# A hybrid mLSTM and neighbourhood-attention block: the z projection channel-major, the conditioning sums in PSUM, the first score blocks spaced, the gate chain split

## The chip, the core and the metric

The kernel runs on one core of one Trainium2 chip. The core has a matrix engine (PE, TensorE), a vector engine (DVE), a scalar engine (ACT), GpSimd (POOL) and a queue engine (SP) that issues most of the DMAs. SBUF is the main on-chip memory; matmuls write into eight banks of PSUM. The metric is the device time of one execution in microseconds (us); lower is better.

## What is computed

One layer over 1024 tokens of width 1024. Every product of real size is done at about float32 accuracy.

```python
cond = silu(c)
shift, scale, gate = split(cond @ w_ada + b_ada, 3)
h = rms_norm(x, norm_gain) * (1 + scale) + shift
proj = h @ w_in          # q_a k_a v_a o_a z_a (1024 each), 16 gates, q_b k_b v_b z_b (512 each), g_merge (2048)
# branch A: 4 heads of 256, bidirectional chunkwise mLSTM
q_a, k_a = split(silu(centred_dwconv(concat(q_a, k_a))))
h_a = sigmoid(o_a) * bidirectional_mlstm(q_a, k_a, v_a, gates)
y_a = rms_norm_per_head(h_a, mlstm_norm_gain) * silu(z_a)
# branch B: 8 heads of 64, neighbourhood attention on a 16 x 64 grid
y_b = neighbourhood_attention(q_b, k_b, v_b, rpb) * silu(z_b)
gm = sigmoid(g_merge + b_merge)
merged = gm[:, 0] * (y_a @ w_proj_a) + gm[:, 1] * (y_b @ w_proj_b)
out = rms_norm(x + gate * (merged @ w_out), final_gain)
```

## The kernel before, in words

Every float32 operand of a large product is split into a rounded high part and a low remainder, and a product is three matmuls: high by high, high by low, low by high (`mm3`). ACT writes the high part, POOL or DVE subtracts it for the low part. `wraw` is a raw weight tile, `whi` and `wlo` its parts, `hhi` and `hlo` the parts of the normalised activations h, kept with channels on the partitions.

A dense product has two forms. The channel-major form (`dense_cm`, and `dense_cm_steps` in the front) holds a 128x128 weight tile stationary and moves 512 tokens past it, so a matmul has 512 columns and the result has channels on the partitions. The token-major form (`dense_tm`) holds 128 tokens of h stationary and moves 256 weight columns, so a matmul has 256 columns and the result has tokens on the partitions. For 256 output channels and the 8 slices of h's channels the first takes 8 x 2 x 2 x 3 = 96 matmuls of 512 columns, the second 8 x 8 x 3 = 192 of 256. Each uses four PSUM banks called `dps`; four more, tag `m`, serve everything small.

The program has five stages.

1. The front (`front`, L239) loads x and the conditioning weights w_ada, normalises and transposes x, and forms shift and scale for eight bands k of 128 channels. For each band a running sum `acc` over eight slices of w_ada is made on DVE (`mod_acc`, L275), one instruction per slice, and PE sums it over the partitions with a matmul against ones (`mod_sum`, L288). `split_at` says how many of the eight slices go through DVE; the others go to PE as matmuls of one column each. `mod_out` makes the vectors `md`, `h_tile` (L329) applies them and writes hhi and hlo. In the same loop PE computes the first query and key projection (`dense_cm_steps`) and the gate projection (`gate_step`, tile `gaps`), band by band. The order of DVE and ACT is written out by hand here, as is that of PE everywhere.
2. Neighbourhood attention (`na_chain`, L692). A chain of 64 blocks (scores, softmax, transposed weights, values) is woven into a stream of dense work. `weave` keeps a count of PE time; each `yield x` of a chain says after how much PE time its next piece may go. The tile `sps` with the scores has a single PSUM buffer, which DVE frees when it writes the normalised weights `pt` (L772).
3. The projection of branch B (`projb`, L833): first one merge gate product (`gmerge`, whose eviction on ACT writes `gtmp`, L828, and sends it to DRAM as `t_d`), then four groups of w_proj_b. Beside it runs the chain `gates` (L502), which makes the mLSTM's decay vectors: scans on DVE up to `M`, `negM` (L543), its copy to DRAM (L544), the decays `dec` on ACT (L547) and their DMAs (L548, L549), and then four vectors that PE transposes (tile `gps`).
4. Branch A (`branch_a`): per head the products k, v, q, then for the head before it `gated_out` (L1068): the o and z products, both token-major. o's eviction multiplies the mLSTM's output `hout`, sums its squares, and after the fourth of four evictions one call of `rsqrt` makes the eight normalising factors `hrstd` (a power on POOL, L236). z's eviction makes `sz` = silu(z) times the normalised hout, and `y_out` (L1097) transposes it, multiplies by the gain and writes it to DRAM (or, for the last head, into the tiles `ya`). The chain of the mLSTM is woven into this stream.
5. The products with w_proj_a and w_out, and the final norm.

Outside the front a scheduler of the framework chooses the order of ACT, DVE, POOL and SP from the program's order and the data's dependences; PE keeps the program's order.

Of the kernel before, what the change touches and what calls it, by code (L numbers as in the profile page):

```python
# [12 lines left out]
F32 = mybir.dt.float32  # L13
F32R = mybir.dt.float32r
AF = mybir.ActivationFunctionType
ALU = mybir.AluOpType
# [3 lines left out]
P = 128  # L20
T = 1024
D = 1024
NK = 8
HEADS = 4
# [17 lines left out]
def f32(ap):  # L42
    return ap.bitcast(F32)


class Build:
# [192 lines left out]
    def front(self, cols):  # L239
# [3 lines left out]
        with self.pool("fr", bufs=2) as fp:  # L243
            wv = io["w_ada"].rearrange("(p j) (s k n) -> p j s k n", j=8, s=3, k=8)
            was, w, xts, accs, md, rs = [], [], [], [None] * NK, [], []
            half = [slice(0, 512), slice(512, T)]

            def load_wa(k):
# [21 lines left out]
                for _ in range(n):  # L270
                    self.transpose(ps, self.ident, self.ident)

            split_at = [8, 0, 8, 7, 8, 8, 8, 8]

            def mod_acc(k, j0, j1):  # L275
                if j0 == 0:
                    accs[k] = fp.tile([P, 2, P], F32, name="acc", bufs=3)
                    nc.vector.tensor_scalar_mul(accs[k], was[k][:, 0], self.cs[:, 0:1])
                for j in range(max(j0, 1), min(j1, split_at[k])):
                    nc.vector.scalar_tensor_tensor(accs[k], was[k][:, j], self.cs[:, j:j + 1], accs[k], op0=ALU.mult, op1=ALU.add)  # L280

            def mod_mix(k, js):
                for j in js:
# [45 lines left out]
            def h_tile(k, s):  # L329
                x, hi, lo, m = xnT[:, k, s], self.hhi[k][:, s], self.hlo[k][:, s], md[k]  # L330
                nc.scalar.activation(x, x, AF.Identity, scale=m[:, 1:2], bias=m[:, 0:1])
                nc.scalar.activation(hi, x, AF.Copy)
                nc.gpsimd.tensor_tensor(lo, x, f32(hi), op=ALU.subtract)  # L333

            def h_high(s):
                x, m = xnT[:, 0, s], md[0]
# [91 lines left out]
            mod_whole(1, 0)  # L428
            copy(7, True)
            mod_whole(1, 1)  # L430
            keep_warm(4, self.psm, "m")
            h_high(half[1])
            split_w(1)
# [66 lines left out]
    def gates(self, gp):  # L500
# [36 lines left out]
        def natural(src, fac):  # L537
            n = gp.tile([36, T], F32, name="nat", bufs=2)
            nc.vector.tensor_scalar_mul(n, src, fac)
            nc.vector.tensor_scalar_mul(n[32:36, ::-1], src[32:36, :], fac)  # L540
            return n
        negM = gp.tile([36, T], F32, name="negM")
        nc.vector.tensor_scalar_mul(negM, M, -1.0)  # L543
        nc.scalar.dma_start(self.negm_d, natural(negM, 1.0))  # L544
        dec = gp.tile([36, NCH], F32, name="dec")
        for c in range(NCH):
            nc.scalar.activation(dec[:, c:c + 1], negM[:, c * L + L - 1:c * L + L], AF.Exp, bias=mc[:, c:c + 1])  # L547
        nc.scalar.dma_start(dec_d, dec)  # L548
        nc.scalar.dma_start(self.decb, dec_d.rearrange("a b -> (a b)").partition_broadcast(P))  # L549
        for i in range(4):  # L550
            if i == 0:
                q = u
            else:
                q = gp.tile([36, T], F32, name="gq", bufs=2)
            if i == 3:
                nc.vector.tensor_tensor(q, b, M, op=ALU.add)
                nc.scalar.activation(q, q, AF.Exp, scale=-1.0)
            for c in range(NCH):
                s = slice(c * L, c * L + L)
                if i == 1:  # L560
                    nc.scalar.activation(q[:, s], u[:, s], AF.Exp, bias=negM[:, c * L + L - 1:c * L + L])
                if i == 2:
                    nc.scalar.activation(q[:, s], negM[:, s], AF.Exp, bias=mc[:, c:c + 1])
            n = natural(q, (1.0, 1.0 / 32, 0.5, 1.0)[i])
            yield 21.0 if i == 0 else 5.0
            ps = self.psm.tile([P, 512], F32, name="gps", tag="m")
            for tt in range(8):
                self.transpose(ps[:, tt * 36:(tt + 1) * 36], n[:, tt * P:(tt + 1) * P], self.ident[0:36, 0:36])
            nc.vector.tensor_copy(self.col[i].rearrange("p a b -> p (a b)"), ps[:, 0:288])
# [116 lines left out]
    def na_chain(self):  # L686

        n = 4 * 16
        heads = {}
        for i in range(n + 3):  # L690
            if i < n:
                pair, hh, b = i // 16, i // 8 % 2, i % 8  # L692
                if b == 0:
                    if hh == 0:
                        if pair == 0:
                            heads[0] = self.na_head(0, 0)
                        yield f"qk{pair}"
                        yield 12.0 if pair == 0 else 6.0
                if (hh, b) == (0, 1) or (hh, b) == (1, 4) and pair < 3:
                    heads[i // 8 + 1] = self.na_head(pair + hh, 1 - hh)  # L700
                self.na_scores(heads[i // 8], b)
                if i % 16 == 15:
                    self.flags.add(f"S{pair}")
                yield NLAG
            if 1 <= i <= n:
                self.na_weights(heads[(i - 1) // 8], (i - 1) % 8)
                yield NLAG
            if i >= 3:
                j = i - 3
                pair = j // 16  # L710
                if j % 16 == 0:
                    yield f"v{pair}"
                    yield 3.2
                    st = self.na_pair[pair]
                    st["v"] = self.np_.tile([P, 8, 2, 2, 64], F32R, name="vb")
                    for h in range(2):
                        self.na_vprep(st, h)
                        yield 1.3
                    yield 1.3
                self.na_values(heads[j // 8], j % 8)  # L720
                if j % 16 == 15:
                    self.flags.add(f"na{pair}")
                yield NLAG
# [312 lines left out]
    def ml_scores(self, mp, c, qh, kh, hd, Pm):  # L1036
# [11 lines left out]
        for dr, row in ((0, rowf), (1, rowb)):  # L1048
# [15 lines left out]
                nc.vector.scalar_tensor_tensor(Dm[:, 1:3], sfl[:, 2:4], 1.0 / 64, Dm[:, 1:3], op0=ALU.mult, op1=ALU.mult)  # L1064
            Pm.append((blocks, self.split(mp, [P, 3, P], Dm, "pm", bufs=2)))

    def gated_out(self, mp, hd):

        nc, io = self.nc, self.io
# [4 lines left out]
        def ev_o(b, ps):  # L1074
            for i in range(2):
# [2 lines left out]
                nc.scalar.activation(so, ps[:, i], AF.Tanh, scale=0.5)  # L1078
                nc.vector.scalar_tensor_tensor(hout[:, tt], so, 1.0, hout[:, tt], op0=ALU.add, op1=ALU.mult)
                nc.scalar.activation(so, hout[:, tt], AF.Square, accum_out=ssq[:, tt:tt + 1])  # L1080
            if b == 3:
                self.rsqrt(rstd, ssq, 1.0 / HD, 4 * EPS, mp, 8)

        def ev_z(b, ps):
            if b % 2 == 0:
                self.sz = mp.tile([P, 2, 2, 256], F32, name="sz", tag="up", bufs=2)
            sz = self.sz[:, b % 2]
            nc.scalar.activation(sz, ps, AF.Tanh, scale=0.5)
            nc.vector.scalar_tensor_tensor(sz, sz, 1.0, ps, op0=ALU.add, op1=ALU.mult)
            for i in range(2):  # L1090
                tt = 2 * b + i
                nc.vector.scalar_tensor_tensor(sz[:, i], hout[:, tt], rstd[:, tt:tt + 1], sz[:, i], op0=ALU.mult, op1=ALU.mult)
            self.spawn(self.y_out(mp, hd, b, sz))
        yield from self.dense_tm(io["w_in"], [(OA + hd * 256, 256)], self.htok, ev_o)
        yield from self.dense_tm(io["w_in"], [(ZA + hd * 256, 256)], self.htok, ev_z)

    def y_out(self, mp, hd, b, sz):  # L1097
        nc = self.nc
        yield 5.0
        tp = self.psm.tile([P, 2, 2, P], F32, name="ytp", tag="m")  # L1100
        for i in range(2):
            for dt in range(2):
                self.transpose(tp[:, dt, i, :], sz[:, i, dt * P:(dt + 1) * P], self.ident)
        s = slice(b * 256, (b + 1) * 256)
        last = hd == HEADS - 1
        if not last:
            yt = mp.tile([P, 2, 256], F32, name="yt", bufs=2)
        for dt in range(2):
            k = hd * 2 + dt
            gain = self.mgain[:, k:k + 1]  # L1110
            if last:
                hi, lo = self.ya[k]
                nc.scalar.activation(hi[:, s], tp[:, dt], AF.Copy, scale=gain)
                nc.vector.scalar_tensor_tensor(lo[:, s], tp[:, dt], gain, f32(hi)[:, s], op0=ALU.mult, op1=ALU.subtract)
            else:
                nc.scalar.activation(yt[:, dt], tp[:, dt], AF.Copy, scale=gain)
                nc.scalar.dma_start(self.ya_d[k][:, s], yt[:, dt])
        if b == 3:
            self.flags.add(f"y{hd}")

    def ml_fill(self, mp):
        gm = [[2], [], [], [3]]
        for hd in range(HEADS):
            yield from self.qkv(mp, hd)
            if hd:
                yield from self.gated_out(mp, hd - 1)
            for g in gm[hd]:
                yield from self.gmerge(0, g)
        yield "ml3"
        yield from self.gated_out(mp, 3)  # L1130

    def branch_a(self):

        nc, io = self.nc, self.io
        with ExitStack() as fs:
# [1 line left out]
            mp = ms.enter_context(self.pool("ml"))  # L1137
            self.mmask = mp.tile([P, 2, P], F32, name="mmask")
            nc.scalar.dma_start(self.mmask, io["mask_ml"])
            self.ml_head = {}  # L1140
            self.spawn(self.ml_chain(mp))

            def fill():
# [193 lines left out]
```

## Time and profile before

| what | value |
|---|---|
| time, median of 3 runs | 1309.07 us (1308.64 to 1310.47) |
| the profiled execution's own time | 1309.19 us |
| its span in the profile | 1307.4 us |
| PE busy | 98% of the span |
| DVE, ACT, POOL busy | 49%, 43%, 32% |

The span runs from the first instruction to the last; the time has 1.8 us more, which lie around it. Matmuls overlap, so a matmul's duration in a row is longer than the distance to the next one. That a PE is 98% busy therefore does not say that it is at its peak. PEclk is the granted clock of TensorE: 1.00 stands for 2.4 GHz and 0.50 for 1.2 GHz.

### The profile page before, as it was taken

How to read it: one execution, taken by the hardware profiler on the slowest of the kernel's cores; microseconds unless marked ns; L12 is line 12 of the kernel's file. 1: busy time of each engine (PE TensorE's matmuls, PEld its weight loads, DVE VectorE, ACT ScalarE, POOL GpSimd, SP SyncE). 2: the span in 40 equal slices, each digit the busy share in tenths (PEclk: the TensorE clock that was granted, in tenths of full speed). 3: DMA queues.
4: the chain of work that ended last, by engine and by line, in shares of the span. 5: the costliest groups of instructions: out<-in, count | busy, mean ns of one | idle time of the engine just before them, and what ended most of it. 6: DMA issues, size and time to landing. Idle time of an engine off the chain costs nothing.

```text
span 1307.4 us, 19858 instructions
## 1 busy us (share of the span) xinstructions
PE 1283.6 (98%) x7560; PEld 1129.6 (86%) x7560; DVE 640.5 (49%) x1381; ACT 564.9 (43%) x1191; POOL 418.0 (32%) x383
## 2 busy tenths in 40 slices
PE   8899999999999999999999999999999999999997
PEld 7678888888888789889989989999989989888886
DVE  6944536445354523356546653465545641533433
ACT  6564435444355313345435543365435543423222
POOL 2653534334346123122212122232212122252332
PEclk9899999999999899999999999999999999999999
DMA  9632222312223462122111221112111123456432
GB/s 291 155 92 83 83 67 82 85 46 84 65 82 129 142 201 60 36 73 49 42 41 41 66 62 44 41 50 71 44 41 41 55 79 93 146 156 202 142 109 85
DMA packets 106187, 116.24 MB, mean 89 GB/s; under 512 B 9724, under 2 KB 86012, under 8 KB 106092
## 3 DMA queue, kind: packets, MB, share of 16 engines
q1 hardware_dynamic: 97352, 102.69, 27.3%
q10 hardware_dynamic: 8740, 12.29, 2.7%
q8 instruction: 59, 0.97, 0.3%
q14 instruction: 36, 0.29, 0.1%
HBM read 92.48 MB, written 20.08 MB: 86 GB/s over the span
## 4 chain that ended last, share of the span: by engine, by line
PE 90%; DVE 4%; DMA 2%; ACT 1%; issue 1%; SPq 1%; POOL 0%; POOLq 0%; ACTq 0%; DVEq 0%
PE dps L79 67%; PE ops L79 8%; PE ips L79 5%; PE sps L79 3%; PE cps L79 3%; PE tps L83 1%; DVE acc L280 1%; DMA t_d<-gtmp 1%; DMA wa<-in_w_ada 1%; PE kps L83 1%; PE ytp L83 0%; SPq L251 0%; DVE M L532 0%; DMA xt<-in_x 0%; DMA ya<-ya_d 0%
## 5 line engine op out<-in xcount | busy, mean ns | idle before, releaser
L74 POOL TENSOR_TENSOR wlo<-wraw,whi 128x512 fp32r<-128x512 f32 x168 | 227.8, 1356 | 577.5 <-ACT whi L73 576.6
L79 PE MATMUL dps<-hhi,whi 128*128 128x512 f32 x768 | 311.8, 406 | 0.8 <-ACT hhi L338 0.5
L79 PE MATMUL dps<-hhi,wlo 128*128 128x512 f32 x768 | 302.6, 394 | 0.0
L79 PE MATMUL dps<-hlo,whi 128*128 128x512 f32 x768 | 299.4, 393 | 0.2 <-POOL hlo L333 0.2
L79 PE MATMUL dps<-whi,hhi 128*128 128x256 f32 x768 | 217.5, 283 | 0.0
L79 PE MATMUL dps<-whi,hlo 128*128 128x256 f32 x768 | 217.4, 283 | 0.0
L79 PE MATMUL dps<-wlo,hhi 128*128 128x256 f32 x768 | 217.4, 283 | 0.0
L73 ACT ACTIVATE whi<-wraw 128x512 fp32r<-128x512 f32 x168 | 105.6, 629 | 229.6 <-PE dps L79 184.6
L79 PEld LDWEIGHTS dps<-hhi,wlo 128*128 128x128 f32 x768 | 145.1, 189 | 32.0
L79 PEld LDWEIGHTS dps<-hhi,whi 128*128 128x128 f32 x768 | 145.5, 189 | 20.2 <-issue 1.7
L79 PEld LDWEIGHTS dps<-hlo,whi 128*128 128x128 f32 x768 | 145.2, 190 | 19.7 <-POOL hlo L333 1.5
L79 PEld LDWEIGHTS dps<-whi,hhi 128*128 128x128 f32 x768 | 147.2, 192 | 0.2
L79 PEld LDWEIGHTS dps<-wlo,hhi 128*128 128x128 f32 x768 | 147.1, 192 | 0.2
L79 PEld LDWEIGHTS dps<-whi,hlo 128*128 128x128 f32 x768 | 147.1, 192 | 0.0
L79 PE MATMUL dps<-ya,whi 128*128 128x512 f32 x256 | 79.4, 392 | 0.0
L769 ACT ACTIVATE sps<-pt,mx 128x384 f32<-128x384 f32 (+1 forms) x64 | 35.7, 558 | 89.8 <-DVE mx L767 89.8
L79 PEld LDWEIGHTS dps<-ya,whi 128*128 128x128 f32 x256 | 47.7, 188 | 9.8 <-DVE t0r L1183 0.3
L1053 POOL TENSOR_TENSOR dg<-negm,mmask 128x256 f32<-128x256 f32 x32 | 24.5, 765 | 98.3 <-issue 28.6
L79 PE MATMUL ops<-woh,mhi 128*128 128x512 f32 (+1 forms) x136 | 51.4, 378 | 0.0
L79 PE MATMUL ops<-woh,mlo 128*128 128x512 f32 (+1 forms) x136 | 51.3, 377 | 0.0
L79 PE MATMUL ops<-wol,mhi 128*128 128x512 f32 (+1 forms) x136 | 51.3, 377 | 0.0
L79 PE MATMUL dps<-ya,wlo 128*128 128x512 f32 x128 | 49.9, 390 | 0.0
(266 smaller groups left out, 2345.8 us busy)
## 6 DMA issues: line engine op xcount, KB each, us to landing
wraw<-in_w_in SPq DMA_DIRECT2D x112, 256.0 KB
wa<-in_w_ada SPq DMA_DIRECT2D x16, 512.0 KB
wraw<-in_w_in SPq DMA_DIRECT2D x64, 128.0 KB
t_d<-gtmp ACTq DMA_DIRECT2D x32, 256.0 KB
xt<-in_x SPq DMA_DIRECT2D x8, 512.0 KB
wag<-in_w_ada SPq DMA_DIRECT2D x16, 256.0 KB
t1r<-t_d SPq DMA_DIRECT2D x8, 512.0 KB
mp_d<-t1r SPq DMA_DIRECT2D x16, 256.0 KB
```

What stands on the lines that cost most here:

```text
L73: nc.scalar.activation(hi, raw, AF.Copy)
L74: nc.gpsimd.tensor_tensor(lo, raw, f32(hi), op=ALU.subtract)
L79: self.nc.tensor.matmul(out, lhsT=lhsT, rhs=rhs, start=start, stop=stop, skip_group_check=True)
L83: self.nc.tensor.transpose(out, src, ident)
L280: nc.vector.scalar_tensor_tensor(accs[k], was[k][:, j], self.cs[:, j:j + 1], accs[k], op0=ALU.mult, op1=ALU.add)
L769: nc.scalar.activation(sv, p_, AF.Exp, bias=mx, scale=-1.0, accum_out=sm)
L1053: nc.gpsimd.tensor_tensor(dg, negm.rearrange("p (a b) -> p a b", a=2), mk, op=ALU.add)
```

## The change

It has four parts, called A to D from here on.

A. In the front, the bands 4 to 7 give their eighth slice to PE (two more one-column matmuls each, one for shift and one for scale). The running sums of the bands from 2 on are kept in a PSUM tile `accp`, one half for even and one for odd bands; the last step of a sum writes the SBUF tile `acc`. The low parts of the bands 6 and 7 are subtracted on DVE and no longer on POOL.

B. In the gate chain a wait of 24 us of PE time stands before negM, and the later 21 is 8. The three DMAs of negM and dec are issued from SP's queue and no longer from ACT's.

C. The chain of neighbourhood attention leaves 2.4, 1.8 and 1.2 us after its first three score blocks, where it left 0.6.

D. z is computed channel-major, before o, into a tile `sz` of its own. rsqrt is called after each of o's evictions, for two factors, and ACT scales hout by them. `y_out` transposes hout, 10 us of PE time later (before: 5), and DVE multiplies the transposed tile by gain and sz.

```diff
-            split_at = [8, 0, 8, 7, 8, 8, 8, 8]
+            split_at = [8, 0, 8, 7, 7, 7, 7, 7]
...
                     accs[k] = fp.tile([P, 2, P], F32, name="acc", bufs=3)
-                    nc.vector.tensor_scalar_mul(accs[k], was[k][:, 0], self.cs[:, 0:1])
+                    parts[k] = run[0][:, k % 2] if k > 1 else accs[k]
+                    nc.vector.tensor_scalar_mul(parts[k], was[k][:, 0], self.cs[:, 0:1])
                 for j in range(max(j0, 1), min(j1, split_at[k])):
-                    nc.vector.scalar_tensor_tensor(accs[k], was[k][:, j], self.cs[:, j:j + 1], accs[k], op0=ALU.mult, op1=ALU.add)
+                    out = accs[k] if j == split_at[k] - 1 else parts[k]
+                    nc.vector.scalar_tensor_tensor(out, was[k][:, j], self.cs[:, j:j + 1], parts[k], op0=ALU.mult, op1=ALU.add)
...
-                nc.gpsimd.tensor_tensor(lo, x, f32(hi), op=ALU.subtract)
+                (nc.vector if k > 5 else nc.gpsimd).tensor_tensor(lo, x, f32(hi), op=ALU.subtract)
...
+            run.append(self.psm.tile([P, 2, 2, P], F32, name="accp", tag="m"))
...
+        yield 24.0
         negM = gp.tile([36, T], F32, name="negM")
         nc.vector.tensor_scalar_mul(negM, M, -1.0)
-        nc.scalar.dma_start(self.negm_d, natural(negM, 1.0))
+        nc.sync.dma_start(self.negm_d, natural(negM, 1.0))
...
-        nc.scalar.dma_start(dec_d, dec)
-        nc.scalar.dma_start(self.decb, dec_d.rearrange("a b -> (a b)").partition_broadcast(P))
+        nc.sync.dma_start(dec_d, dec)
+        nc.sync.dma_start(self.decb, dec_d.rearrange("a b -> (a b)").partition_broadcast(P))
...
-            yield 21.0 if i == 0 else 5.0
+            yield 8.0 if i == 0 else 5.0
...
-                yield NLAG
+                yield NLAG if i > 2 else 2.4 - NLAG * i
...
+    def z_path(self, mp, hd):
+        nc, io = self.nc, self.io
+        def evac(a, h, banks):
+            if a == 0 and h == 0:
+                self.sz[hd] = mp.tile([P, 2, T], F32, name="sz", tag="sz")
+            sz = self.sz[hd][:, a, h * 512:h * 512 + 512]
+            nc.scalar.activation(sz, banks[h], AF.Tanh, scale=0.5)
+            nc.vector.scalar_tensor_tensor(sz, sz, 1.0, banks[h], op0=ALU.add, op1=ALU.mult)
+        yield from self.dense_cm(io["w_in"], [(ZA + hd * 256, 256)], self.hT, evac)
...
-            if b == 3:
-                self.rsqrt(rstd, ssq, 1.0 / HD, 4 * EPS, mp, 8)
-
-        def ev_z(b, ps):
...
-                nc.vector.scalar_tensor_tensor(sz[:, i], hout[:, tt], rstd[:, tt:tt + 1], sz[:, i], op0=ALU.mult, op1=ALU.mult)
-            self.spawn(self.y_out(mp, hd, b, sz))
+            s = slice(2 * b, 2 * b + 2)
+            self.rsqrt(rstd[:, s], ssq[:, s], 1.0 / HD, 4 * EPS, mp, 2)
+            for tt in (2 * b, 2 * b + 1):
+                nc.scalar.activation(hout[:, tt], hout[:, tt], AF.Copy, scale=rstd[:, tt:tt + 1])
+            self.spawn(self.y_out(mp, hd, b, hout))
...
-        yield 5.0
+        yield 10.0
...
-                self.transpose(tp[:, dt, i, :], sz[:, i, dt * P:(dt + 1) * P], self.ident)
+                self.transpose(tp[:, dt, i, :], hout[:, 2 * b + i, dt * P:(dt + 1) * P], self.ident)
...
+            nc.vector.scalar_tensor_tensor(yt[:, dt], tp[:, dt].rearrange("p i t -> p (i t)"), gain, self.sz[hd][:, dt, s], op0=ALU.mult, op1=ALU.mult)
             if last:
                 hi, lo = self.ya[k]
-                nc.scalar.activation(hi[:, s], tp[:, dt], AF.Copy, scale=gain)
-                nc.vector.scalar_tensor_tensor(lo[:, s], tp[:, dt], gain, f32(hi)[:, s], op0=ALU.mult, op1=ALU.subtract)
+                nc.scalar.activation(hi[:, s], yt[:, dt], AF.Copy)
+                nc.vector.tensor_tensor(lo[:, s], yt[:, dt], f32(hi)[:, s], op=ALU.subtract)
             else:
-                nc.scalar.activation(yt[:, dt], tp[:, dt], AF.Copy, scale=gain)
                 nc.scalar.dma_start(self.ya_d[k][:, s], yt[:, dt])
```

In `ml_fill` the call of `z_path` for a head stands right before its `gated_out`, which now does o alone; that of the last head stands before the hold `"ml3"`, which waits for the last mLSTM chunk.

On DVE in the front, the sums of the bands 3 to 5 before (`acc` is the running sum of a band, `md` a band's finished vectors; the sums of two bands take turns):

```order
L280 SCALAR_TENSOR_TENSOR acc<-wa,cs,acc 128x256 x6
L278 TENSOR_SCALAR acc<-wa,cs 128x256
L303 TENSOR_TENSOR md<-mps,b_ada_c_sb 128x1
L304 SCALAR_TENSOR_TENSOR md<-mps,b_ada_c_sb 128x1
L305 TENSOR_TENSOR md<-md,norm_gain_sb 128x1
L280 SCALAR_TENSOR_TENSOR acc<-wa,cs,acc 128x256 x7
```

The same place after the change, and at the end the last sum of band 7 with what follows it:

```order
L283 SCALAR_TENSOR_TENSOR accp<-wa,cs,accp 128x256 x3
L280 TENSOR_SCALAR accp<-wa,cs 128x256
L306 TENSOR_TENSOR md<-mps,b_ada_c_sb 128x1
L307 SCALAR_TENSOR_TENSOR md<-mps,b_ada_c_sb 128x1
L308 TENSOR_TENSOR md<-md,norm_gain_sb 128x1
L283 SCALAR_TENSOR_TENSOR accp<-wa,cs,accp 128x256 x2
L283 SCALAR_TENSOR_TENSOR acc<-wa,cs,accp 128x256
...
L283 SCALAR_TENSOR_TENSOR acc<-wa,cs,accp 128x256
L336 TENSOR_TENSOR hlo_103<-xnT,hhi_102 128x512 x2
```

A band has seven sum instructions rather than eight, six of them without two SBUF operands; the two subtractions for band 6 stand behind the last sum.

On ACT where branch B's projection begins, before (`dec` needs negM, `gq` is the second gate vector, the DMA of `negm_d` needs the tile `nat`):

```order
L547 ACT_TABLE_LOAD
L547 ACTIVATE dec<-negM,mc 36x1 x4
L561 ACTIVATE gq<-gate_4124,negM 36x256
L548 DMA dec_d<-dec 36x4
L544 DMA negm_d<-nat 36x1024
L828 ACTIVATE gtmp<-dps,bmh 128x512
L549 DMA decb<-dec_d 128x144
L829 DMA t_d<-gtmp 128x512
L828 ACTIVATE gtmp<-dps,bmh 128x512
```

And after the change:

```order
L552 ACT_TABLE_LOAD
L552 ACTIVATE dec<-negM,mc 36x1 x4
L566 ACTIVATE gq<-gate_4129,negM 36x256
L833 ACTIVATE gtmp<-dps,bmh 128x512 x2
L834 DMA t_d<-gtmp 128x512 x2
```

The three DMAs are gone from the queue; the four `dec` and the first `gq` still stand ahead of the first `gtmp`. On PE the transposes of the first gate vector, which stood behind 6 matmuls of w_proj_b, stand behind 60.

On ACT around o's evictions of the last head, before (`so` is sigmoid's tanh, the second instruction squares hout):

```order
L1078 ACTIVATE so<-dps 128x256 x2
L1080 ACTIVATE so,hssq<-hout 128x256 x2
```

And after:

```order
L1095 ACTIVATE so<-dps 128x256 x2
L1097 ACTIVATE so,hssq<-hout 128x256 x2
L1095 ACTIVATE so<-dps 128x256 x2
L1101 ACTIVATE hout<-hout,hrstd 128x256 x2
```

Two scalings of hout per eviction, which need the power on POOL, now stand in ACT's queue between the evictions.

## Rows read from the trace of the kernel before

**Rows 1.** The page's first part: busy time, share of the span, instructions.

```profile
PE 1283.6 (98%) x7560; PEld 1129.6 (86%) x7560; DVE 640.5 (49%) x1381; ACT 564.9 (43%) x1191; POOL 418.0 (32%) x383
```

**Rows 2.** PE's waits: waiting instruction, releaser, us in total, times, longest.

```profile
PE mps L291 <- DVE acc L280: 6.3, 5, 2.1
PE sps L79 <- DVE pt L772: 2.5, 3, 1.2
PE dps L79 <- ACT gtmp L828: 1.8, 1, 1.8
```

**Rows 3.** The chain that ended last, in time order: start, us, what.

```profile
20.13 7.25 DMA wa<-in_w_ada
...
146.86 16.33 PE dps L79 x72
...
1077.44 42.85 PE dps L79 x358
```

**Rows 4.** PE's timeline in the front: start, us, instruction, idle before and releaser.

```profile
39.17 0.38 PE L291 MATMUL mps<-ones,acc 128*128 128x1 f32 x2 [1.93 <-DVE acc L280]
...
47.02 0.50 PE L291 MATMUL mps<-ones,acc 128*128 128x1 f32 x4
...
58.03 0.61 PE L291 MATMUL mps<-ones,acc 128*128 128x1 f32 x4 [2.07 <-DVE acc L280]
58.50 0.47 PE L79 MATMUL gaps<-hhi,gw 128*128 128x512 f32 x1
...
63.48 0.61 PE L291 MATMUL mps<-ones,acc 128*128 128x1 f32 x4 [1.07 <-DVE acc L280]
...
73.58 0.39 PE L79 MATMUL dps<-hhi,whi 128*128 128x512 f32 x1
```

**Rows 5.** DVE instructions by tile: ns min/median/max, first and last start.

```profile
L280 DVE SCALAR_TENSOR_TENSOR acc<-wa,cs,acc x48: 472/484/1523, 13.4 to 62.9; 128x256 f32<-128x256 f32 x48
...
L1092 DVE SCALAR_TENSOR_TENSOR sz<-hout,hrstd,sz x32: 467/479/1530, 739.7 to 1128.6; 128x256 f32<-128x256 f32 x32
...
L1089 DVE SCALAR_TENSOR_TENSOR sz<-sz,dps x16: 672/684/690, 738.9 to 1125.7; 128x512 f32<-128x512 f32 x16
```

**Rows 6.** DVE's timeline in the front.

```profile
44.02 4.93 DVE L280 SCALAR_TENSOR_TENSOR acc<-wa,cs,acc 128x256 f32<-128x256 f32 x7
```

**Rows 7.** POOL's timeline over the same stretch.

```profile
45.69 2.97 POOL L333 TENSOR_TENSOR hlo<-xnT,hhi 128x512 fp32r<-128x512 f32 x2 [2.07 <-ACT hhi L332]
```

**Rows 8.** SP's timeline: an issue of w_ada, and the first after branch B's weights.

```profile
29.52 1.76 SPq L251 DMA_DIRECT2D wa<-in_w_ada  x1
...
446.73 0.34 SPq L852 DMA_DIRECT2D mp_d<-t1r  x1
```

**Rows 9.** Two windows: us, busy PE, PEld, DVE, ACT, POOL, PEclk, DMA, GB/s.

```profile
39.50:46.40 6.90, 6.90 (x21) 5.65 (x21) 6.79 (x13) 3.99 (x7) 4.72 (x4) 0.51 1.14 284
435.50:442.30 6.80, 6.80 (x22) 5.05 (x22) 1.47 (x3) 4.18 (x9) 0.00 (x0) 0.50 0.59 164
```

**Rows 10.** PE's timeline at the second and third score blocks.

```profile
88.81 0.44 PE L79 MATMUL sps<-kB,qA 128*128 128x384 f32 x1 [1.18 <-DVE pt L772]
...
91.78 0.45 PE L79 MATMUL sps<-kB,qA 128*128 128x384 f32 x1 [0.75 <-DVE pt L772]
```

**Rows 11.** ACT's timeline where branch B's projection begins.

```profile
434.24 0.69 ACT L828 ACTIVATE gtmp<-dps,bmh 128x512 f32<-128x512 f32 x1 [1.14 <-DVE nat L540]
...
434.95 0.37 ACTq L829 DMA_DIRECT2D t_d<-gtmp  x1
...
439.00 0.69 ACT L828 ACTIVATE gtmp<-dps,bmh 128x512 f32<-128x512 f32 x1 [2.55 <-DMA t_d<-gtmp]
```

**Rows 12.** PE's timeline at the same place.

```profile
434.98 0.50 PE L79 MATMUL dps<-ybhi,whi 128*128 128x512 f32 x1 [1.82 <-ACT gtmp L828]
```

**Rows 13.** A window of branch A, ACT alone: us, busy ACT, PEclk, DMA, GB/s.

```profile
683.00:780.00 97.00, 51.79 (x126) 1.00 0.20 55
```

**Rows 14.** POOL's timeline at the last head's normalising factors.

```profile
1103.89 1.65 POOL L236 TENSOR_TENSOR hrstd<-rsq,mhalf 128x8 f32<-128x8 f32 x1
```

More of the change, by code (lines that the diff above doesn't have):

```diff
@@ L245, in front @@
             was, w, xts, accs, md, rs = [], [], [], [None] * NK, [], []
+            parts, run = [None] * NK, []
             half = [slice(0, 512), slice(512, T)]
@@ L1080, in ev_o, with y_out @@
                 nc.scalar.activation(so, hout[:, tt], AF.Square, accum_out=ssq[:, tt:tt + 1])
-            if b == 3:
-                self.rsqrt(rstd, ssq, 1.0 / HD, 4 * EPS, mp, 8)
-        def ev_z(b, ps):
[L1085 to L1091, printed above, removed]
-                nc.vector.scalar_tensor_tensor(sz[:, i], hout[:, tt], rstd[:, tt:tt + 1], sz[:, i], op0=ALU.mult, op1=ALU.mult)
-            self.spawn(self.y_out(mp, hd, b, sz))
+            s = slice(2 * b, 2 * b + 2)
[3 more added lines that the diff above has]
+            self.spawn(self.y_out(mp, hd, b, hout))
         yield from self.dense_tm(io["w_in"], [(OA + hd * 256, 256)], self.htok, ev_o)
-        yield from self.dense_tm(io["w_in"], [(ZA + hd * 256, 256)], self.htok, ev_z)
-    def y_out(self, mp, hd, b, sz):
+    def y_out(self, mp, hd, b, hout):
         nc = self.nc
-        yield 5.0
+        yield 10.0
         tp = self.psm.tile([P, 2, 2, P], F32, name="ytp", tag="m")
@@ L1102, in y_out @@
             for dt in range(2):
-                self.transpose(tp[:, dt, i, :], sz[:, i, dt * P:(dt + 1) * P], self.ident)
+                self.transpose(tp[:, dt, i, :], hout[:, 2 * b + i, dt * P:(dt + 1) * P], self.ident)
         s = slice(b * 256, (b + 1) * 256)
         last = hd == HEADS - 1
-        if not last:
-            yt = mp.tile([P, 2, 256], F32, name="yt", bufs=2)
+        yt = mp.tile([P, 2, 256], F32, name="yt", bufs=2)
         for dt in range(2):
@@ L1125, in ml_fill @@
             if hd:
+                yield from self.z_path(mp, hd - 1)
                 yield from self.gated_out(mp, hd - 1)
@@ L1128, in ml_fill @@
                 yield from self.gmerge(0, g)
+        yield from self.z_path(mp, HEADS - 1)
         yield "ml3"
@@ L1139, in branch_a @@
             nc.scalar.dma_start(self.mmask, io["mask_ml"])
-            self.ml_head = {}
+            self.ml_head, self.sz = {}, {}
             self.spawn(self.ml_chain(mp))
```

## The prediction, made before the changed kernel ran

> **What bounds the kernel now.** The page's first part comes first: PE is busy 98% of the span, the other engines about half of it or less [rows 1]. So only three kinds of change can pay: fewer PE microseconds, less PE idle time, or a higher clock. Next come PE's waits by releaser: DVE's sums in the front cost 6.3 us in five waits, the first score blocks 2.5 in three, one eviction in branch B's projection 1.8 [rows 2]. The chain of waits runs through PE nearly throughout. Its long pieces give the true distance of matmuls, since the duration of one overlaps the next: 16.33/72 = 0.2268 us for 512 columns, 42.85/358 = 0.1197 for 256 [rows 3]. Windows come last: in two stretches of about 6.9 us the granted clock is half, 1.2 rather than 2.4 GHz [rows 9]. Each follows a PE wait (1.93 us until 39.17, 1.82 until 434.98) [rows 4, 12], and each gives away about half its length, 3.4 us.
>
> **Part A, the front.** The five waits are for `acc`. A sum instruction takes 0.48 us at the median but up to 1.52 [rows 5]; seven of them took 4.93 us while POOL wrote hlo for 2.97 us [rows 6, 7]. The tile list points at the cause: `sz` at L1092, whose two large inputs are both in SBUF, reaches 1.53 us, while L1089, on twice the columns but with one input in PSUM, never exceeds 0.69 [rows 5]. With the running sum in PSUM I expect the long ones to go. The new instruction itself is not shown: 0.35 from below (half of 0.69), 0.69 from above; I take 0.48, the same step on SBUF.
>
> From the sum matmul at 58.03 to that at 63.48 lie 5.45 us, of which 1.07 are idle and about 0.16 the drain of the last matmul (0.39 long, 0.23 apart): 4.2 us of PE work per band [rows 4]. The two sums of a band cost 58.50 - 58.03 = 0.47; two more matmuls of that size make a band 4.7 us on PE. DVE has seven sum steps and three short ones, 7 x 0.48 + 0.4 = 3.8, so PE sets the pace unless a step exceeds about 0.62.
>
> The earlier waits stay: band 4's weights, issued at 29.52 [rows 8], land after about 7.25 us [rows 3], near 36.8, and DVE's first product of band 4 stands in its queue ahead of band 2's vectors, with or without the change. Hence I expect PE idle until about 38.9 again, the half clock after it, and the sum of band 4 at about 46.8 (now 47.02). From there three bands at 4.7 reach band 7's sum at 60.9 (now 63.48). Its own two added matmuls cost 0.47, and the 10.1 us to the next dense product (63.48 to 73.58) [rows 4] stay: it starts at 71.5, or at 70.8 if the small waits in those 10.1 go too. Gain 2.1 to 2.8; I take 2.5. Lower end: the long steps stay, the bands keep today's pace and the 0.47 comes on top, gain -0.5. Upper end: the clock no longer falls, 2.5 + 3.4 = 5.9. The subtractions of bands 6 and 7 stand on DVE behind the last sums; POOL took 1.48 us for one [rows 7], DVE's form with two SBUF operands 0.48 for half the columns, so h is ready no later and they cost nothing; if DVE were late there, the front's last products would wait about 1 us, which the lower end covers.
>
> **Part C, the score blocks.** The second block's scores wait 1.18 us for the single score bank, the third's 0.75; their distance is 2.97 us [rows 10], and the three waits add to 2.5 [rows 2]. Now 12 matmuls of 0.2268 stand between the first two blocks in place of 3, as many between the next two and 9 between the two after them: 2.7 us, with the block's own 0.45 more than 2.97, and 2.0 with scores and transposes about 2.9. Gain 2.4 (2.0 to 2.5). The dense work spent here is missing later in the chain, where PE has no such wait; if it runs out there, up to 2.4 comes back.
>
> **Part D, z.** 768 matmuls of 256 columns become 384 of 512: 768 x 0.1197 = 91.9 against 384 x 0.2268 = 87.1, gain 4.8. Among other small matmuls the 512 ones stand wider apart, in the front (4.2 - 0.47)/16 = 0.233: 89.5, gain 2.4. I take 4.0.
>
> The Trainium skill, "TensorE: Matmul & The Clock Gate", section "Back-to-back issue gap", speaks against this: it gives a lone matmul N/2.4 plus 2.5 ns at any N, by which halving the count saves 384 x 2.5 ns, an estimate of 1.0 us. The rows have 0.1197 where it has 0.109, and 0.2268 where it has 0.216, so the cost per matmul here is larger.
>
> What hangs on o's eviction: ACT now scales hout by factors that DVE and then POOL must make, four times per head. One power on POOL for eight factors took 1.65 us [rows 14]. ACT is busy 51.8 of 97 us in such a stretch [rows 13], so a wait of 1 to 3 us in its queue delays the next eviction or weight split, but not PE as long as banks and weights are ahead. I charge 0.4 for it (0 to 20, the upper end in R4). The extra PE time before the transposes (10 us rather than 5) only moves them among other dense work.
>
> **Part B, the gate chain.** PE waited 1.82 us for the first `gtmp` [rows 12], and this stood 1.14 us behind a DMA in ACT's queue that needed `nat` [rows 11]. The three DMAs leave that queue; on SP, which issues its next one only at 446.73 [rows 8], they cost nothing. So the wait falls to about 0.7, not to nothing, since `dec` and `gq` still stand ahead. But the third gtmp waits for the DMA of the first (434.95 to 439.00) [rows 11]. All of it starts 1.1 earlier, so the third bank is free at 439.00 + 0.69 - 1.1 = 438.6, while PE, which starts at 433.9 and needs it after 12 matmuls of 0.2268, arrives at 436.6. Before, slow matmuls and the gate transposes filled that time; now the transposes come 60 matmuls later. Loss before 1.8 + 3.4 (clock) = 5.2; after 0.7 + 2.0, plus 0 to 3.4 of clock. Gain -0.9 to 2.5, and 5.2 if both waits are hidden; I take 1.2.
>
> **Sum.** 2.5 + 2.4 + 4.0 + 1.2 - 0.4 = 9.7 us off the profiled execution's 1309.19 (its span of 1307.4 and 1.8 around it): 1299.5. That execution is 0.12 above the median of the runs, so I forecast 1299.4.
>
> **Rivals.**
>
> R1, both half-clock stretches go. Then A, B and D give 5.9, 5.2 and 4.8, with C 18.3: 1290.8. For it: each stretch follows a wait of under 2 us. Against: the first hangs on a load that the change doesn't move, and in branch B two waits remain.
>
> R2, the sums in PSUM are no quicker. A gives -0.5 and the rest 7.2: 1302.4. For it: 0.69 us is over the 0.62 that PE's pace allows. Against: that row has twice the columns.
>
> R3, a matmul costs nearly the same per column at both sizes. z saves 1.0 in place of 4.0: 1302.4. Against it stand the two distances, taken over 72 and 358 matmuls [rows 3].
>
> R4, the slower side: the power in ACT's path. At each of o's 16 evictions ACT waits for DVE and then POOL; where POOL is inside a subtraction of 1.48 us [rows 7], the wait is up to 1.48 + 1.65 = 3.1. The kernel is slower than before once more than 10.1/16 = 0.63 us of each reaches PE; at 1.2 it is 1309.1 + 19.2 - 10.1 = 1318. For it: the dense products share four banks, and ACT frees each and splits each weight. Against: ACT idles nearly half of that stretch [rows 13].
>
> R5, the gate chain doesn't do what it says: the third bank's wait brings the half clock back in full. B then gives -0.9 in place of 1.2: 1299.4 + 2.1 = 1301.5, inside the forecast's own range.
>
> **Chances.** The forecast has 0.63 (own range 1295 to 1303, R5 in it), R1 0.15, R2 0.11, R3 0.06, R4 0.05. The range 1290.5 to 1304 takes in R2, R3 and half of R1; outside are R4, the rest of R1 and a tail of the forecast, 0.17. A measurement of this kernel tells 0.2%, 2.6 us, from no change. Faster than 1306.5 is all but R4 and tails of R2 and R3: 0.90; within 0.2%: 0.05; slower: 0.05.
>
> **What would show it.** Front: `accp` steps near 0.48 with no long ones, no PE wait for sums after band 3, the next dense product between 70.8 and 71.5; R2 if the steps exceed 0.62. Scores: no wait on pt in the first three blocks. z: about 22 us of dense 512-column matmuls per head. Branch B: a wait of about 0.7 on the first gtmp and 2.0 on the third, which in turn waits for t_d. Branch A: PE waits on ACT `so` or `hout` stay under 0.1 us each, or else R4. The forecast is wrong where the clock shows a new half-speed stretch, or where both of the old ones are gone.

## The result, and the profile after

The changed kernel takes 1301.25 us (median of 4 runs, 1299.68 to 1302.65) against 1309.48 before (1308.64 to 1310.47): the ratio is 0.9937, 95% interval 0.9919 to 0.9954. The forecast was 1299.4, with 1290.5 to 1304.0 as its range. The gain is 8.2 us where 9.7 were expected, but it is made of other pieces. Its profiled execution took 1302.65 us, a span of 1300.9. It is the slowest of the four, and so is the profiled one of only_a, only_d, split_only, b_gt3, tail and best among its runs: a trace can hold waits that the median run does not have.

The page's first part, to be held against [rows 1]: PE is busy 6.5 us less, with 368 matmul records fewer (384 fewer by z, 16 more by the sums, whose matmuls are two records each).

```profile
PE 1277.1 (98%) x7192; PEld 1107.8 (85%) x7192; DVE 643.5 (49%) x1393; ACT 566.6 (44%) x1199; POOL 417.2 (32%) x391
```

PE's waits after the change, the rows that answer to [rows 2] and the new ones:

```profile
PE dps L79 <- ACT gtmp L833: 2.9, 2, 2.0
PE dps L79 <- ACT so L1095: 2.7, 2, 1.4
...
PE mps L294 <- DVE acc L283: 2.0, 3, 0.7
...
PE dps L79 <- DVE qA L663: 0.8, 1, 0.8
PE ops L79 <- DVE mlo L1197: 0.8, 1, 0.8
PE sps L79 <- DVE pt L777: 0.8, 2, 0.4
...
PE ops L79 <- DVE t0r L1192: 0.7, 1, 0.7
...
PE dps L79 <- DVE kl L666: 0.4, 1, 0.4
```

The waits for `acc` fell from 6.3 to 2.0 us and those for `pt` from 2.5 to 0.8. The wait for `gtmp` grew, and three are new: 2.7 us for `so`, the evictions of o; 1.2 us for `qA` and `kl`, the evictions of the query and key products right behind the front; and 1.5 us in all before the first w_out matmuls (`t0r`, `mlo`).

PE's timeline of the front, where [rows 4] stood:

```profile
38.75 0.38 PE L294 MATMUL mps<-ones,acc 128*128 128x1 f32 x2 [0.74 <-DVE acc L283]
...
44.26 0.38 PE L294 MATMUL mps<-ones,acc 128*128 128x1 f32 x2 [0.68 <-DVE acc L283]
...
53.50 0.28 PE L294 MATMUL mps<-ones,acc 128*128 128x1 f32 x2
...
58.07 0.28 PE L294 MATMUL mps<-ones,acc 128*128 128x1 f32 x2
...
69.19 0.47 PE L79 MATMUL dps<-hhi,whi 128*128 128x512 f32 x1 [0.84 <-DVE qA L663]
```

The sum of band 4 is at 44.26 (before 47.02), from band 6 to band 7 lie 4.57 us without a wait (before 5.45), and the next dense product starts at 69.19 instead of 73.58.

The sum instructions by tile, for [rows 5]; columns as there:

```profile
L283 DVE SCALAR_TENSOR_TENSOR accp<-wa,cs,accp x31: 475/490/491, 28.1 to 55.0; 128x256 f32<-128x256 f32 x31
L280 DVE TENSOR_SCALAR accp<-wa,cs x6: 487/488/490, 27.6 to 50.1; 128x256 f32<-128x256 f32 x6
L283 DVE SCALAR_TENSOR_TENSOR acc<-wa,cs,accp x6: 481/481/484, 31.9 to 55.5; 128x256 f32<-128x256 f32 x6
```

Not one exceeds 0.491 us, where the SBUF form reached 1.523. All 11 sum steps above 0.7 us in the kernel before lie beside a subtraction on POOL, for about 1.1 us or more; after the change 26 of 44 steps lie beside POOL's work, and none is long. Only the first step of a band got dearer: 0.488 into PSUM, 0.356 into SBUF in the same execution.

Three windows, with the columns of [rows 9]: a half-clock stretch, and the two places that had one before.

```profile
30.10:36.90 6.80, 6.27 (x17) 4.59 (x16) 5.07 (x15) 3.25 (x8) 3.73 (x7) 0.50 0.98 250
39.50:46.40 6.90, 6.22 (x32) 5.01 (x32) 5.74 (x15) 3.94 (x6) 5.11 (x5) 1.00 1.18 293
429.00:435.80 6.80, 4.75 (x21) 3.56 (x20) 2.85 (x4) 3.41 (x8) 0.00 (x0) 1.00 0.64 161
```

Ahead of the two stretches of [rows 9] the kernel before ran a third at half clock, which neither those rows nor the prediction count:

```profile
29.30:32.70 3.40, 2.80 (x8) 1.69 (x6) 3.22 (x9) 0.53 (x1) 1.18 (x1) 0.50 1.02 228
```

Between the first matmuls and 442 us it thus ran three, 17.1 us together; now there is one of 6.8.

Where the 6.5 us between the two spans came from, by the start of the first matmul of a stage in the PE timelines:

| starts at | before | after | difference so far |
|---|---|---|---|
| dense product after the front | 73.58 | 69.19 | -4.4 |
| w_proj_b | 434.98 | 428.55 | -6.4 |
| branch A | 485.38 | 478.27 | -7.1 |
| w_proj_a | 1123.34 | 1112.15 | -11.2 |
| w_out | 1213.00 | 1205.32 | -7.7 |
| end of the span | 1307.40 | 1300.86 | -6.5 |

Up to w_proj_a the change had gained 11.2 us. It gives back 3.5 in w_proj_a and 1.1 in w_out.

### The profile page after: what moved, and what is told of

It is laid out like the page before. It is cut to its first block, busy times and chain, and to the rows that moved or that the text cites. A ratio compares the mean times of both kernels' runs of the same rounds, so it can differ in the third digit from the quotient of the medians.

```text
span 1300.9 us, 19151 instructions
## 1 busy us (share of the span) xinstructions
PE 1277.1 (98%) x7192; PEld 1107.8 (85%) x7192; DVE 643.5 (49%) x1393; ACT 566.6 (44%) x1199; POOL 417.2 (32%) x391
## 4 chain that ended last, share of the span: by engine, by line
PE 86%; DMA 4%; DVE 3%; ACT 3%; issue 2%; POOL 1%; SPq 1%; POOLq 0%; DVEq 0%; ACTq 0%
PE dps L79 63%; PE ops L79 8%; PE ips L79 5%; PE sps L79 3%; PE cps L79 3%; PE tps L83 1%; DMA wa<-in_w_ada 1%; DMA t_d<-gtmp 1%; DMA wor<-in_w_out 1%; PE ytp L83 1%; PE kps L83 1%; DMA xt<-in_x 0%; POOL mpr L1193 0%; DMA ya<-ya_d 0%; PE gaps L79 0%
## 5 line engine op out<-in xcount | busy, mean ns | idle before, releaser
L79 PE MATMUL dps<-hhi,whi 128*128 128x512 f32 x896 | 361.7, 404 | 3.0 <-ACT hhi L341 1.4
L79 PE MATMUL dps<-hhi,wlo 128*128 128x512 f32 x896 | 352.1, 393 | 0.0
L79 PE MATMUL dps<-hlo,whi 128*128 128x512 f32 x896 | 348.7, 392 | 0.0
L79 PEld LDWEIGHTS dps<-hlo,whi 128*128 128x128 f32 x896 | 169.3, 189 | 22.7 <-DVE hlo L345 0.4
L79 PE MATMUL dps<-wlo,hhi 128*128 128x256 f32 x512 | 144.7, 283 | 0.0
L79 PE MATMUL dps<-whi,hlo 128*128 128x256 f32 x512 | 144.6, 283 | 0.0
L79 PE MATMUL dps<-whi,hhi 128*128 128x256 f32 x512 | 144.6, 282 | 0.0
L79 PEld LDWEIGHTS dps<-wlo,hhi 128*128 128x128 f32 x512 | 97.9, 191 | 0.3
L79 PEld LDWEIGHTS dps<-whi,hhi 128*128 128x128 f32 x512 | 97.9, 191 | 0.3
L79 PEld LDWEIGHTS dps<-whi,hlo 128*128 128x128 f32 x512 | 97.9, 191 | 0.0
L1058 POOL TENSOR_TENSOR dg<-negm,mmask 128x256 f32<-128x256 f32 x32 | 23.9, 746 | 84.9 <-issue 40.3
```

Of the source, the lines that this page charges most:

```text
L79: self.nc.tensor.matmul(out, lhsT=lhsT, rhs=rhs, start=start, stop=stop, skip_group_check=True)
L1058: nc.gpsimd.tensor_tensor(dg, negm.rearrange("p (a b) -> p a b", a=2), mk, op=ALU.add)
```

## The experiments

Each part was put alone on the kernel before, the parts A and B were taken to pieces, and four kernels try repairs (b_gt3 on the kernel before; tail, tail_gt3 and best on the change). Every group of runs had runs of the kernel before on the same chip beside it (medians 1309.8, 1309.4 and 1309.2). The ratio pairs each kernel with those; the median difference is given too, since the two disagree by up to 1.1 us.

| kernel | median us | ratio to before, 95% interval | difference of medians |
|---|---|---|---|
| only_a | 1305.79 | 0.9961 [0.9947, 0.9975] | -4.0 |
| only_b | 1308.01 | 0.9982 [0.9973, 0.9990] | -1.8 |
| only_c | 1307.68 | 0.9982 [0.9973, 0.9990] | -1.7 |
| only_d | 1306.16 | 0.9965 [0.9952, 0.9978] | -3.7 |
| psum_only | 1305.04 | 0.9963 [0.9949, 0.9977] | -4.4 |
| split_only | 1309.59 | 1.0002 [0.9992, 1.0011] | +0.2 |
| b_dma | 1307.47 | 0.9992 [0.9983, 1.0001] | -1.8 |
| b_gt3 | 1307.90 | 0.9993 [0.9984, 1.0002] | -1.3 |
| tail | 1299.99 | 0.9917 [0.9902, 0.9932] | -9.8 |
| tail_gt3 | 1297.31 | 0.9900 [0.9885, 0.9916] | -12.1 |
| best | 1298.25 | 0.9915 [0.9901, 0.9928] | -11.0 |

**Part A alone (only_a):** the hunks of the front, the rest as before.

> Part A alone on the kernel before. Theory 1 (the trace of the changed kernel is typical): the PSUM sums take 0.49 us each, the two long waits of 1.9 and 2.1 us go and with them one of the two half-clock stretches of the front, so the next dense product starts at about 69 us instead of 73.6 and nothing later gives it back: about 1304.8 us, ratio 0.9965. Rival (the first half-clock stretch of the changed kernel came from another part or from chance): the product starts at 71 to 71.5 as predicted, gain 2.5, about 1306.9, ratio 0.998.

Its next dense product starts at 69.05, and the time falls by 4.0: theory 1 by its figures. Its mechanism came in part: of the two long waits one stayed (1.85 us, until 37.96). And which half-clock stretches go varies: this execution had 3.4 us from 28.9 and 3.4 from 39.2, the changed kernel 6.8 from 30.1.

**Part A in two pieces (psum_only, split_only):** the first keeps `split_at = [8, 0, 8, 7, 8, 8, 8, 8]` and POOL's hlo, the second is

```diff
-            split_at = [8, 0, 8, 7, 8, 8, 8, 8]
+            split_at = [8, 0, 8, 7, 7, 7, 7, 7]
```

> Of part A only the sums in PSUM; all eight slices of the bands 4 to 7 stay on DVE and hlo stays on POOL. Theory 1 (the long steps beside POOL were the cause): eight steps of 0.49 and the vectors are 4.4 us a band on DVE, beside 4.2 on PE; the next dense product starts at 69.5 to 71, at least 3 of part A's gain of about 4.5. Rival (the number of steps was the cause): less than half of it, later than 71.5.

> Of part A only the eighth slice of the bands 4 to 7 given to PE; the sums stay in SBUF and hlo on POOL. Theory 1 (the long steps beside POOL were the cause): each band saves one step of 0.5 on DVE and adds 0.47 on PE, two or three steps a band stay at 1.4 to 1.5, the product starts at 71.5 to 73, gain 0.5 to 2. Rival (the number of steps): 69.5 to 71, gain 3 or more.

psum_only starts the next product at 68.72 and has the whole gain, although 10.2 us of its front ran at half clock, as much as in the kernel before; split_only starts it at 74.18 and has none. The tile list of split_only still has the long steps:

```profile
L280 DVE SCALAR_TENSOR_TENSOR acc<-wa,cs,acc x44: 472/485/1539, 13.6 to 62.7; 128x256 f32<-128x256 f32 x44
```

So the number of steps was not the limit; the steps that stretch beside POOL were. In split_only the gain is even below the expected 0.5: PE pays 0.47 a band, and this saves no long step (all 11 are still there).

The third piece of part A, hlo of the bands 6 and 7 on DVE, was not run alone. The waits for `qA` and `kl` (0.84 and 0.45 us in the changed kernel) stand in all five profiles that have it and in none of the eight that do not, psum_only among them. So it probably costs about 1 us of PE time, where the prediction had put it at nothing; that was not tested.

**Part C alone (only_c):**

```diff
-                yield NLAG
+                yield NLAG if i > 2 else 2.4 - NLAG * i
```

> Part C alone on the kernel before. Theory 1: the three waits for pt (2.5 us) go and nothing takes their place, 2.4 us, ratio 0.998. Rival (the dense work spent early is missing later): in the changed kernel two new waits for pt of about 0.57 us stand near 130 and 378 us, so half of it comes back, 1.3 us, ratio 0.999.

1.7 by medians, 2.4 by the ratio. The three early waits for `pt` are gone and one of 0.4 is left:

```profile
PE sps L79 <- DVE pt L772: 0.4, 1, 0.4
```

That speaks for theory 1; the rival's 1.3 is not excluded.

**Part B alone and in pieces (only_b, b_dma, b_gt3).** b_dma moves only the DMAs, b_gt3 only adds a buffer:

```diff
-        nc.scalar.dma_start(self.negm_d, natural(negM, 1.0))
+        nc.sync.dma_start(self.negm_d, natural(negM, 1.0))
...
-            t = self.ev.tile([P, 512], F32, name="gtmp", tag="e1")
+            t = self.ev.tile([P, 512], F32, name="gtmp", tag="e1", bufs=3)
```

> Part B alone on the kernel before. Theory 1: PE's first wait for gtmp falls from 1.8 to 0.85 us, a second of about 2.05 appears on the third gtmp, and the half-clock stretch there goes (3.4 us): net gain about 2, 1307.4, ratio 0.9985. Rival: the second wait brings the half clock back, net 0.9 slower, 1310.3, ratio 1.0006.

> Of part B only the three DMAs moved to SP's queue; both waits of the gate chain as before. Theory 1 (the DMA of negM in ACT's queue held up the first gtmp): PE's first wait falls from 1.8 to about 0.7, and with the gate transposes still close behind, the wait for the third bank is 1 or less: 1307.5 to 1308.5, as much as part B in whole (1.8 of 1.8). Rival (the moved transposes matter): 1309, less than half of it.

> The kernel before with three buffers for gtmp (and for ztmp and t0r) and nothing else. Theory 1 (two causes, one behind the other): the wait for the DMA of negM stays, 1.8 us and the half clock after it with it, so it gains less than 1 us, 1308.5 to 1309.5; three buffers pay only with the DMAs gone. Rival (the two buffers were the only limit): the whole 2.7 us that it gave on the tail kernel, 1306.7.

Part B gives 1.8 alone, and the DMAs 1.8 of it by medians (their ratio alone is too wide to say). The rival of only_b, 1310.3, is excluded: no half clock came there. PE's waits in b_dma are 0.56 for the first bank and 0.71 for the fourth, 18 matmuls later:

```profile
433.22 0.50 PE L79 MATMUL dps<-ybhi,whi 128*128 128x512 f32 x1 [0.56 <-ACT gtmp L828]
...
439.19 0.50 PE L79 MATMUL dps<-ybhi,whi 128*128 128x512 f32 x1 [0.71 <-ACT gtmp L828]
```

The gate transposes, moved away in part B, had filled part of that time: with them gone only_b waits 0.56, 0.21 and 1.52, on the first, third and fourth bank, and the changed kernel 0.85 and 2.05, on the first and third. So the DMAs bring what gain there is, and the moved transposes add none that shows; by the ratios neither b_dma nor b_gt3 is clear of no change. b_gt3 surprised: with a third buffer the scheduler puts one gtmp ahead of the negM DMA, and the first wait falls to 0.73 without any DMA moved; 1.21 stay on the fourth bank. Its expectation that the wait for the DMA of negM stays was wrong.

**Part D alone (only_d):** z channel-major and what belongs to it.

> Part D alone on the kernel before. Theory 1: branch A up to the first matmul of w_proj_a is 4 to 5 us shorter, but w_proj_a then waits about 1.4 us twice for the banks of the last head's o, whose evictions stand on ACT behind the power on POOL, and the start of w_out waits another 1 to 2 us: net between -1.5 and +0.5 us, 1308 to 1310, ratio 0.999 to 1.000. Rival (the waits in w_proj_a and w_out of the changed kernel come from the shifted loads or other parts): net gain of 4, 1305.4, ratio 0.997.

It gains 3.7, the rival's figure. Branch A is 4.3 us shorter (from 485.41 to 1119.07, before 485.38 to 1123.34), and the wait for so is there, but once, not twice:

```profile
PE dps L79 <- ACT so L1090: 1.4, 1, 1.4
```

Theory 1 had the place right and put too much into it. The trace itself took 1307.88 us, only 1.3 less than that of the kernel before: 4.3 less in branch A, 1.4 more for so and 1.9 more at the start of w_out. The waits at the start of w_out belong to no part: only_a had 1.7 us of them, only_b 1.4, only_c 1.5 and only_d 1.9, all at code that none of them touches; what sets them was not tested.

**The last head (tail).** The changed kernel, with one power and all scalings of the last head after its fourth eviction:

```diff
+            if hd == HEADS - 1 and b < 3:
+                return
+            done = range(4) if hd == HEADS - 1 else (b,)
+            s = slice(2 * done[0], 2 * b + 2)
+            self.rsqrt(rstd[:, s], ssq[:, s], 1.0 / HD, 4 * EPS, mp, 2 * len(done))
+            for d in done:
+                for tt in (2 * d, 2 * d + 1):
+                    nc.scalar.activation(hout[:, tt], hout[:, tt], AF.Copy, scale=rstd[:, tt:tt + 1])
+                self.spawn(self.y_out(mp, hd, d, hout))
```

> The changed kernel, but for the last head the power and the scaling of hout come once, after all four evictions of o. Theory 1 (the scalings that wait for POOL hold up the next eviction, and so the bank): the two waits of 1.4 us for so in w_proj_a fall below 0.5 each, about 1298.5 us, 2.5 below the changed kernel. Rival (ACT itself is too slow there, with its other work, or the wait moves to the transposes and the last tiles of ya): waits of the same sum elsewhere, 1301, no change against the changed kernel.

The two waits fall from 2.7 to 1.0 us (0.8 and 0.2, where below 0.5 each was expected):

```profile
PE dps L79 <- ACT so L1095: 1.0, 2, 0.8
```

1299.99 is 1.3 under the changed kernel, measured in another group of runs; the intervals overlap. What is left of the wait stands behind conversions of `ya`, which the scheduler puts between the evictions.

**A third buffer for gtmp (tail_gt3), and eight slices again (best):**

> The tail kernel, with three buffers in place of two for gtmp (and for the two other tiles of that tag, ztmp and t0r). Theory 1: the third gtmp no longer waits for the DMA of the first, PE's wait of 2.0 to 2.3 us there falls below 0.3, time 1.8 to 2.2 us under the tail kernel's. Rival: ACT's gate vectors or the bank itself hold the eviction as long, less than 0.5.

> The tail_gt3 kernel with all eight slices of the bands 4 to 7 on DVE again, the sums in PSUM and hlo as in the change. Theory 1 (the split gave nothing): PE has 8 one-column matmuls fewer (0.47 us per band, 1.9 us) while DVE's 4.4 us per band stays beside PE's 4.2; the next dense product starts 0.3 to 1.3 earlier, 1296.0 to 1297.0. Rival (at that pace DVE sets it, with waits at the sums of 0.3 or more a band): no gain or 0.5 slower, 1297.3 to 1297.8.

tail_gt3 takes 1297.31, 2.7 under tail in other runs; PE's wait for gtmp is one of 0.6 us, for the first bank, where the tail kernel had 2.9 in two:

```profile
PE dps L79 <- ACT gtmp L833: 0.6, 1, 0.6
```

It is the fastest kernel here and beats the kernel before and the change: ratio 0.9900 [0.9885, 0.9916] to before, against 0.9937 for the change. best, with 8 matmuls fewer, is not shown to be faster or slower: the intervals overlap, and from its first dense matmul at 21.70 to the next dense product at 70.32 it takes 48.6 us, tail_gt3 from 20.76 to 68.85 takes 48.1. The rival's waits at every sum are not there. PE waits once, for band 4:

```profile
46.17 0.61 PE L294 MATMUL mps<-ones,acc 128*128 128x1 f32 x4 [1.74 <-DVE acc L283]
```

tail_gt3 waits 0.69 there. From this sum to that of band 7, first in best and then in tail_gt3 (columns of [rows 9]):

```profile
46.20:60.30 14.10, 14.10 (x60) 11.49 (x61) 12.84 (x31) 9.42 (x15) 10.50 (x9) 0.88 0.51 121
43.90:57.70 13.80, 13.80 (x72) 11.80 (x73) 11.54 (x29) 10.62 (x17) 11.40 (x9) 1.00 0.51 129
```

best spent 3.4 of these 14.1 us at half clock, from 47.0. At full clock its bands stand 4.1 to 4.2 us apart (51.98, 56.12, 60.30), those of tail_gt3 4.57. So the eight slices do save PE 0.4 us a band, as theory 1 says, and the longer wait at band 4 and the half clock behind it took this back. Whether that half clock belongs to the kernel or to the execution is open; psum_only had the same wait (1.73) and the same stretch behind it.

## Why the prediction was right, and where its steps were not

The time was right, 1301.25 in 1290.5 to 1304, because two wrong sizes of opposite sign met: part A brought more than forecast, and the last head's evictions cost more. That is luck, and the range of 13.5 us left room for it. Of the prediction's own signs, those for the `accp` steps and for the two gtmp waits came. Against it, PE still waited for a sum behind band 3 (0.68 us), the next dense product started at 69.19 rather than 70.8 to 71.5, PE waited 1.37 us twice for so where it allowed 0.1, and both half-clock stretches that it named are gone.

**Part A was too small: 2.5 forecast, 4.0 measured alone.** The mechanism held: steps of 0.49 (forecast 0.48), none long, 4.6 us a band (4.7). The step that failed was "PE idle until about 38.9 again, the half clock after it, and the sum of band 4 at about 46.8". PE did wait until 38.75, for 0.74 us rather than 1.93, and no half clock followed there; the sum of band 4 came at 44.26. The half-clock stretch of this execution had begun at 30.1, ahead of that wait, and only shortened it. I had read the stretches of one execution as fixed, and they are not (below). The missing half clock makes about half of the 2.5 us by which band 4's sum came before 46.8: in only_b and only_c, whose front is that of the kernel before, no half clock followed the wait either, and the sum came at 45.74 and 45.52, behind a wait of 2.2 for DVE. The other half is the quicker steps, which I had credited only behind band 4. The 10.1 us after band 7's sum were also there (58.07 to about 68.2), with the wait of 0.84 for `qA` behind them. That the subtractions moved to DVE "cost nothing" is the other step that failed, as far as the profiles tell (above). The gain is that of the sums and not of the clock: from band 3's sum to band 7's the seven kernels with sums in SBUF take 23.9 to 24.7 us, and the six with sums in PSUM 19.3 to 20.7. That the two added matmuls were needed at all was not questioned; split_only and best show no gain from them.

**Part C was about right:** 2.4 forecast, 1.7 alone by medians and 2.4 by the ratio.

**Part D was right alone and too high in company: 3.6 forecast with its charge of 0.4, 3.7 alone.** z's gain in branch A is 4.1 to 4.3. The step that failed is that a wait in ACT's queue delays the next eviction, "but not PE as long as banks and weights are ahead", with a charge of 0.4: for the last head the banks are not ahead. ACT's timeline there, after the change:

```profile
1112.82 0.63 ACT L1095 ACTIVATE so<-dps 128x256 f32<-128x256 f32 x2
1114.23 0.91 ACT L1101 ACTIVATE hout<-hout,hrstd 128x256 f32<-128x256 f32 x2 [0.78 <-POOL hrstd L236]
...
1115.85 0.62 ACT L1095 ACTIVATE so<-dps 128x256 f32<-128x256 f32 x2
1117.25 0.91 ACT L1101 ACTIVATE hout<-hout,hrstd 128x256 f32<-128x256 f32 x2 [0.78 <-POOL hrstd L236]
...
1118.86 0.63 ACT L1095 ACTIVATE so<-dps 128x256 f32<-128x256 f32 x2
```

And PE's, in the same stretch:

```profile
1116.53 0.73 PE L79 MATMUL dps<-ya,whi 128*128 128x512 f32 x2 [1.37 <-ACT so L1095]
...
1119.54 0.73 PE L79 MATMUL dps<-ya,whi 128*128 128x512 f32 x2 [1.37 <-ACT so L1095]
```

Evictions come 3.0 us apart (1112.82, 1115.85, 1118.86), of which 0.78 is the wait for the power and 0.91 the scaling. PE needs a bank each 6 x 0.2268 = 1.4 us. That is rival R4's mechanism; it decided at two of its 16 places, because behind the first three heads comes dense work that waits for nothing, and behind the last one w_proj_a wants the banks at once. The prediction does not ask when w_proj_a needs them. Moving the power out (tail) takes 1.7 of the 2.7 away.

**Part B: both waits came as worked out,** 0.85 forecast as 0.7 and 2.05 as 2.0, the second on the third gtmp, held by its DMA. The half clock after them did not come (1.00 in the third window above), so the net 1.2 became 1.8 alone. It is not ruled out: the tail kernel, with the same part B, ran 3.4 us at half clock from 435.6, behind its second wait of 2.28.

**The sum.** The four parts alone add to 11.2 us by medians (4.0, 1.8, 1.7, 3.7) and to 14.4 by the ratios (5.1, 2.4, 2.4, 4.6); the whole gave 8.2 by either. In the profiles the wait for so is 1.3 longer with all parts than in only_d, that for gtmp 0.6 longer than in only_b, and that for pt 0.4 longer than in only_c: 2.3 of the missing 3.0 to 6.2. The rest is open. Why so waits twice in company and once alone shows on ACT. The last head's first eviction starts 1.87 us before w_proj_a's first matmul in the changed kernel (1110.28, 1112.15) and 3.64 before it in only_d (1115.43, 1119.07), so that there the third eviction is late too. In ACT's queue a conversion of `ya` stands right ahead of that first eviction; it waited 2.04 us for its load in the changed kernel and 0.28 in only_d.

**The rivals.** R1's condition came in the profiled execution, and its time did not: both stretches that the prediction names are gone, though the load that I had named against it did not move, while the one it does not name grew from 3.4 to 6.8 us. R1 put 3.4 us on each stretch. But in the front DVE's sums set the pace: from band 3's sum to band 7's the kernel before took 24.31 us with 6.8 of it at half clock, only_b 24.33 with 3.4. And in branch B's projection the half clock had hidden a wait for the third bank, which was 1.34 us in only_c, where the same code ran at full clock. R2 (steps over 0.62) and R3 (z saves 1.0) are refuted, by 0.49 us and by 4.1 to 4.3 us in branch A. By the gap of a lone matmul in the Trainium skill, "TensorE: Matmul & The Clock Gate", section "Back-to-back issue gap", it would have been 1.0, an estimate; the trace does not agree. R5 did not come in the changed kernel.

## What to carry to other kernels

Look for the long tail of an instruction, not its median: here the same step took 0.48 or 1.5 us, and putting one of two large operands into PSUM removed the tail, while fewer steps did nothing. When a product's eviction gets a longer chain, ask who wants its PSUM banks next, at each place where the loop ends as well as inside it. A wait that goes is worth its own length only as far as the next one behind it on the same banks: gtmp's second buffer stood right behind the DMA that was moved away.

## What the runs showed of the hardware

The half-clock stretches move between kernels that are the same up to that point: in all profiles here they came in lengths of 3.4 or 6.8 us, between 6.8 (after, tail_gt3) and 17.1 us (before, only_d, psum_only) in sum ahead of w_proj_b's middle. Where w_proj_b begins, they mostly went with the wait. Six kernels wait 1.8 to 2.1 us for the first `gtmp`, and in four of them (before, only_a, only_d, psum_only) 6.8 us at half clock began within 1 us of its end; in the seven that wait 0.85 us or less none began there. At half clock the matmuls of 512 columns in the front stood 0.43 us apart, at full clock 0.23, so a stretch of 3.4 us costs at most about 1.6 us, an estimate, and little where PE is waiting anyway. The spread of a kernel's own runs is in small part that at most: over the 61 runs of the kernel before, time and mean granted clock go together only weakly (correlation -0.41).
